# A hybrid decoder step on one core: a unit's output before the next unit's joining, an inversion with fewer DMAs, a projection by halves

## The chip, the core and the metric

One core of a Trainium2 chip runs one launch of the kernel. The metric is device time of that launch in microseconds (us). The engines named below are TensorE (PE, matmul, with its weight loads PEld), VectorE (DVE), ScalarE (ACT), GpSimd (POOL) and SyncE (SP). SyncE and ScalarE issue DMAs, each in the order of its own queue.

## The reference

One layer of a decoder, for a prompt of 1024 tokens and 8 samples of 8 tokens, width 1024. A combined projection `w_in` feeds two mixers: A is RWKV-7 with 8 heads of 64, B a chunked gated delta rule with 4 heads of 128. Their outputs go through `w_o`, a layer norm, a ConvFFN of width 2816, a second layer norm, and a gated embedding of each layer, `p @ w_ple`, with an RMS norm.

```python
proj = x @ w_in
o_a, a_shift_new, a_wkv_new = _rwkv7_mix(proj[..., :A_SHIFT_W], ...)
o_b, b_conv_new, b_ssm_new = _gated_delta_mix(proj[..., A_SHIFT_W:], ...)
mix = jnp.concatenate([o_a, o_b], axis=-1) @ w_o
x = _layer_norm(DN_ALPHA * x + mix, ln1_g, ln1_b)
ffn, f_conv_new = _conv_ffn(x, f_conv, w_up, f_conv_w, f_conv_b, w_down)
x = _layer_norm(DN_ALPHA * x + ffn, ln2_g, ln2_b)
e = _rms_norm(p @ w_ple, ple_g)
x = x + jax.nn.sigmoid(x @ w_ple_gate) * e
```

Both mixers solve, for each chunk of tokens, a lower triangular system with ones on its diagonal: `sol = triangular_solve(eye + Lmat, rhs)`. The kernel inverts these matrices.

## The kernel before

All matrix products are made in three matmuls: each operand is split into a high and a low part (`split`, L257: ScalarE makes the high part at L217, a subtraction at L220 the low one), and high by high, high by low and low by high are accumulated. Weight chunks of 128x512 come from `wchunk` (L385), through the ring `wraw` of 4, on SyncE's queue. The accumulators are four PSUM banks `acc`; mixing uses two banks `aux` and two `scan`. Banks and other rings are given out in the order of the program.

The program is written as one long list, and a scheduler lays it out over the engines' queues ahead of time, by priority and by its own estimate of when each instruction is ready. On the chip each queue then runs strictly in its order. Work written inside `fill()` has a far lower priority: it is taken where nothing else is ready by the estimate.

The mixing is cut into ten units: eight prompt units (tb, half, g), each 256 tokens and one group of heads, numbered 0 to 7 below, and two sample units. A unit passes through these steps:

- `prep` (L1047): loads of the projected rows, convolutions, norms on TensorE (`aux<-tmp,cst`), gram matrices `MG` and `MB`, and at its end `invert`.
- `invert` (L947): 24 matrices of 64x64 per prompt unit. ScalarE's queue (`s.uq`) writes them to DRAM (`inv_t`), then loads the 16x16 diagonal blocks to `iN`, one block per partition, in 4 DMAs (L963). VectorE inverts all 96 blocks at once in 14 steps on `iN`, `iY` and `it`. The result and its transpose go back to DRAM (`inv_x`, `inv_y`), 96 rows of 1 KB each, and from there in 16 DMAs of 16 partitions (L992) to the diagonal blocks of `Dd` and `Dt`, which were cleared once in `setup` (L318).
- `merge` (L996), the joining: four rounds of small matmuls that make the inverse of the 64x64 matrices from the inverted blocks, then three steps that join pairs to 128x128. Each round takes both `aux` banks and begins with `touch` (L204), a matmul of 8 columns that takes the waits of the round (`aux<-zeros`); in rounds 0 and 1 it waits for the loads of `Dt` and `Dd`.
- `scan` (L1069): the chunks one after another, with the state. `scan` gets the joining of the next unit as `ahead` and runs it through `together` in turn with its own steps.
- `mix_out` (L1087): `out` (L899) norms and gates the result, with `aux` banks (`aux<-OA,cst` first), and stores two halves to `od` on SyncE's queue (L928, L934).

The loop in `run` (L1653) goes, for unit i: scan i with the joining of i+1, output i, then `prep` of i+2. Fill: the projections of the second 512 tokens, the embeddings' projection `ple` (L1369), then after unit 3 `dense_first` with `w_o`, which loads `od` of units 0 to 3 and keeps its input order, `norm_first` at normal priority, and the FFN of the first 512 tokens. When the mixing is done, the second 512 tokens and the samples follow, with the FFN in `ffn_second`.

`ple` computes two halves of the columns for each of two blocks of 512 tokens: `dense` runs over 2 weight chunks and 4 token tiles, fills four `acc` banks at once and copies them out at the end. Both `load_x`, `ple`, `ffn_second` and `transposed` put part of the low parts of their splits on GpSimd.

Of the kernel before, what the change touches and what calls it, by code (L numbers as in the profile page):

```python
# [145 lines left out]
class Kern:  # L146
# [109 lines left out]

    def split(s, hi, lo, raw, eng=None):  # L257

        s.act(hi, raw)
        s.tt(lo, raw, hi.bitcast(F32), ALU.subtract, eng or s.nc.gpsimd)  # L260

# [10 lines left out]
    def setup(s):  # L272
# [43 lines left out]
        s.DX = [s.tl([128, 12, LB], "DX%d" % i) for i in range(2)]  # L316
        for t in (s.Dd, s.Dt, *s.DX):
            nc.gpsimd.memset(t, 0.0)  # L318
        for g in range(2):
            for S in (s.SA, s.SB):  # L320
                S.append(s.tl([128, 2, 128], "S%d%d" % (g, S is s.SB)))
                nc.gpsimd.memset(S[g], 0.0)
# [33 lines left out]
    def load_x(s, src, more=None):  # L356

        x = s.xtiles()
        if not more and not s.late:
            for k in range(0, KT, 2):  # L360
                raw = s.tl([128, D], "X", 3, dt=F32R, pool=s.c0).bitcast(F32).rearrange("p (k t) -> p k t", k=2)
                s.nc.sync.dma_start(raw, src[:, k:k + 2, :])
                s.split(x[k // 2][:, 0], x[k // 2][:, 1], raw, s.nc.vector if k < 4 else None)
            return x
        for k in range(KT):
            raw = s.hraw() if s.late else s.st()
            with s.tc.high_priority() if more and k < 1 else ExitStack():
                s.nc.sync.dma_start(raw, src[:, k, :])
                s.split(*s.xk(x, k), raw, s.nc.vector if more else None)
                if more and k % 2 == 0:  # L370
                    more(k)
        return x

    def load_xs(s):
        x = s.tl([128, D], "X", 3, dt=F32R, pool=s.c0).rearrange("p (k i t) -> p k i t", k=KT, i=2)
        raw = s.tmp(128, KT, 64)

        def load(k):
            ks = slice(k, k + 2)
            s.nc.sync.dma_start(raw[:, ks], s.I["xT"][:, ks, T:T + 64])  # L380
            s.split(x[:, ks, 0, :], x[:, ks, 1, :], raw[:, ks], s.nc.vector)

        return x, load

    def wchunk(s, src, to=None):  # L385

        w = src.shape[-1]
        raw = s.wraw()
        hi, lo = to or (s.tl([128, 512], t, 3, dt=F32R, pool=s.mp) for t in ("whi", "wlo"))
        with s.tc.high_priority():  # L390
            s.nc.sync.dma_start(raw[:, :w], src)
            s.split(hi[:, :w], lo[:, :w], raw[:, :w], s.nc.vector)
        return hi, lo
# [545 lines left out]
    def systems(s, sa, sb):  # L939

        for h in range(2):
            r = 64 * h
            yield h, 0, sa["MG"].rearrange("p c a s e t -> p (c a) s e t")[r:r + 64, :, 0, 1 - h, :]
            if r < sb["L"]:
                yield h, 2 * sa["nch"], sb["MB"][r:r + 64, :, :, 0, r:r + 64].rearrange("p q h t -> p (q h) t")

    def invert(s, sa, sb, small):  # L947

        nc = s.nc
        nch = sa["nch"]  # L950
        nb = 2 * sb["nq"]
        nh = 2 * nch + nb
        ns = nh + (2 * nch if small else nh)
        dT = s.tl([64, 24, 64], "inv_t", 2, pool=s.dp)
        d1, d2 = (s.tl([96, 16, 16], t, 2, pool=s.dp) for t in ("inv_x", "inv_y"))
        N, Y, tmp = s.iN, s.iY, s.it
        DX = s.DX[0]
        s.DX = s.DX[::-1]
        for h, y, t in s.systems(sa, sb):
            s.uq.dma_start(dT[:, h * nh + y:h * nh + y + t.shape[1], :], t)  # L960
        n = 4 * ns
        for k in range(4):
            s.uq.dma_start(N[k * ns:(k + 1) * ns], dT[16 * k:16 * k + 16, :ns, 16 * k:16 * k + 16].rearrange("r y t -> y r t"))  # L963
        nc.vector.tensor_copy(Y[:n], N[:n])
        for j in range(1, 15):
            m = 15 - j
            y = Y[:n, 0:j]
            t = tmp[:n, :j * m].rearrange("p (c i) -> p c i", c=j)
            s.mul(t, N[:n, j:j + 1, j + 1:].broadcast_to([n, j, m]), y[:, :, j:j + 1].broadcast_to([n, j, m]))
            s.add(y[:, :, j + 1:], y[:, :, j + 1:], t)  # L970
        nc.vector.memset(Y[:n].rearrange("p a b -> p (a b)")[:, 0::17], 1.0)
        s.uq.dma_start(d1[:n], Y[:n])
        if small:
            nc.gpsimd.memset(DX, 0.0)
            todo = ((DX, d1, 64),)
        else:
            nc.vector.tensor_copy(N[:n], Y[:n].rearrange("p c i -> p i c"))
            s.uq.dma_start(d2[:n], N[:n])
            todo = ((s.Dt, d2, 0), (s.Dd, d1, 0))
        for D, d, w in todo:  # L980
            for h in range(2):
                for k in range(4):
                    rows = slice(64 * h + 16 * k, 64 * h + 16 * k + 16)
                    cols = slice(w * h + 16 * k, w * h + 16 * k + 16)
                    y = k * ns + h * nh
                    if small:
                        s.uq.dma_start(D[rows, :2 * nch, cols], d[y:y + 2 * nch].rearrange("y r t -> r y t"))
                        if h == 0:
                            y += 2 * nch
                            s.uq.dma_start(D[rows, 8:8 + nb, cols], d[y:y + nb].rearrange("y r t -> r y t"))  # L990
                    else:
                        i = s.uq.dma_start(D[rows, :, cols], d[y:y + nh].rearrange("y r t -> r y t"))  # L992
                        sa.setdefault("dma", []).append(i.ins)
        sa["DX"] = sb["DX"] = DX

    def merge(s, sa, sb):  # L996
# [8 lines left out]
        for k in range(4):  # L1005
            bs = [s.bank() for _ in range(2)]
            with s.inrow():
                s.touch(bs[0], s.nc.cur_bb.bb.instructions[-1], *(sa["dma"][8 * k:8 * k + 8] if k < 2 else ()))
                for i in range(12):
# [58 lines left out]

    def scan(s, tb, half, g, st, ahead):  # L1069

# [4 lines left out]
        def a_all():  # L1075
            for c in range(NCH):
                yield from s.a_step(sa, c, OA)
                yield
# [4 lines left out]

        s.together(a_all(), b_all(), *ahead)
        return OA, OB
# [240 lines left out]
    def transposed(s, xs, i, c0, x, tag, dst=None):  # L1326
# [5 lines left out]
        for k in range(0, KT, q):  # L1332
# [18 lines left out]
            s.act(hi, u)  # L1351
            s.tt(lo, u, hi.bitcast(F32), ALU.subtract, s.nc.gpsimd if (k // q) % 2 else None)

# [15 lines left out]
    def ple(s):  # L1369
        nc, I = s.nc, s.I  # L1370
        for tb in range(3):
# [12 lines left out]
            for h in range(2):  # L1384
# [6 lines left out]
                def evac(t, b):  # L1391
# [3 lines left out]

                s.dense(2, (lambda i: x[i]) if x else None, lambda i: I["w_ple"][h][:, i, :], evac,
                        None if x else (lambda i: xs[:, i]), lambda v: out(8, 64, v))

# [210 lines left out]
    def run(s):  # L1609
# [14 lines left out]
        with s.tc.tile_pool(name="c0", bufs=1) as c0:  # L1624
            s.c0 = c0
            with s.tc.tile_pool(name="mix", bufs=1) as p:
# [26 lines left out]
                for i, u in enumerate(units):  # L1653
                    o = s.sample_scan(*u, st[i]) if len(u) == 1 else s.scan(*u, st[i], [s.merge(*st[i + 1][:2])] if len(units[i + 1]) == 3 else [])
                    if len(u) == 1:
                        s.sample_out(*u, st[i], o)
                    else:
                        s.mix_out(*u, st[i], o)
                    if i == 3:
                        with s.fill():  # L1660
# [73 lines left out]
```

## Time and profile before

| | us |
|---|---|
| median of 3 runs (1918.12 to 1926.15) | 1921.58 |
| profiled execution | 1920.4 |
| its span, first to last instruction | 1918.6 |
| TensorE busy in the span | 1831.8 |
| mean granted TensorE clock | 0.989 of full |

The profile is one execution, read by views: the page with busy time of each engine; windows, which give the same for any stretch; waits, which name who waited for whom; and timelines, which give instructions in order of time, with the idle time before each in brackets and what ended it. Times are counted from the span's start. In names, `out<-in` is what an instruction writes and reads; for a matmul the moving operand stands before the stationary one. A `q` behind an engine is its queue, that is a DMA issue there.

### The profile page before, as it was taken

Reading aid. Unit: us, or ns where it says so; the run is one execution under the profiler, and the core shown is the slowest. Engines: PE = TensorE matmul, PEld = TensorE weight load, DVE = VectorE, ACT = ScalarE, POOL = GpSimd, SP = SyncE. Lnnn points to the kernel's source line nnn. Section 1 sums busy time; section 2 is a strip of 40 time slices with the busy share of each in tenths; the row PEclk is TensorE's granted clock in tenths of the full one; section 3 lists DMA queues with packets and bytes.
Section 4 is the critical chain, followed back from the end, with each engine's and each line's share of the span. In section 5 each row is a group of like instructions: output and inputs, shape, how many; then the busy total and the mean of one; then the engine's idle time right before and its main releaser. Section 6 shows DMA issues by size and latency. Waiting matters only on the chain. (4 is left out here: it accounts for less than half of the span.)

```text
span 1918.6 us, 29879 instructions
## 1 busy us (share of the span) xinstructions
PE 1831.8 (95%) x10446; PEld 1463.3 (76%) x10446; DVE 1269.8 (66%) x2748; ACT 918.0 (48%) x1814; POOL 154.7 (8%) x305
## 2 busy tenths in 40 slices
PE   9999999999799798999999999999999999999998
PEld 7878777777567577777887767777787888888877
DVE  4366566758586685877768767666857752455488
ACT  5454447465564744646455435543633332333372
POOL 2000010001000000000000000200212210111000
PEclk9999999999899899999999999999999999999999
DMA  6435342434444365442423446875332222222355
GB/s 216 152 123 153 112 113 89 137 100 133 144 138 145 126 181 163 129 114 82 117 81 112 131 137 194 274 246 200 134 119 92 96 78 83 83 78 79 114 174 165
DMA packets 219126, 255.88 MB, mean 133 GB/s; under 512 B 81848, under 2 KB 117096, under 8 KB 218976
## 3 DMA queue, kind: packets, MB, share of 16 engines
q1 hardware_dynamic: 162040, 246.36, 39.8%
q10 hardware_dynamic: 56936, 7.62, 2.5%
q8 instruction: 82, 1.34, 0.3%
q14 instruction: 68, 0.56, 0.1%
HBM read 200.64 MB, written 53.26 MB: 132 GB/s over the span
## 5 line engine op out<-in xcount | busy, mean ns | idle before, releaser
L190 PE MATMUL acc<-x,whi 128*128 128x512 f32 x2400 | 784.5, 403 | 7.9 <-ACT whi L217 5.1
L220 DVE TENSOR_TENSOR wlo<-wraw,whi 128x512 fp32r<-128x512 f32 (+1 forms) x462 | 323.2, 700 | 343.7 <-ACT whi L217 319.0
L217 ACT ACTIVATE whi<-wraw 128x512 fp32r<-128x512 f32 (+1 forms) x462 | 287.4, 623 | 497.8 <-PE acc L190 169.0
L190 PEld LDWEIGHTS acc<-x,whi 128*128 128x128 f32 x2400 | 429.5, 189 | 89.0 <-issue 7.8
L190 PE MATMUL acc<-x,wlo 128*128 128x512 f32 x1200 | 483.0, 403 | 0.0
L190 PEld LDWEIGHTS acc<-x,wlo 128*128 128x128 f32 x1200 | 226.9, 189 | 54.3 <-issue 6.0
L190 PE MATMUL acc<-whi,X 128*128 128x512 f32 x436 | 145.5, 407 | 9.5 <-ACT st L217 6.2
L217 ACT ACTIVATE st<-acc 128x512 f32<-128x512 f32 (+2 forms) x134 | 77.4, 595 | 62.3 <-PE acc L190 39.2
L190 PEld LDWEIGHTS acc<-whi,X 128*128 128x128 f32 x436 | 81.9, 191 | 29.8 <-ACT st L217 7.2
L190 PE MATMUL acc<-wlo,X 128*128 128x512 f32 x220 | 87.5, 398 | 0.0
L229 DVE SCALAR_TENSOR_TENSOR st<-st,par,st 128x512 f32<-128x512 f32 (+1 forms) x132 | 78.1, 593 | 2.8
L217 ACT ACTIVATE st<-st 128x512 f32<-128x512 f32 x66 | 33.3, 505 | 72.9 <-DVE st L229 68.4
L190 PE MATMUL scan<-whi,X 128*128 128x256 f32 (+2 forms) x208 | 62.4, 335 | 0.0
L217 ACT ACTIVATE tmp<-tmp 128x512 f32<-128x512 f32 (+4 forms) x75 | 40.5, 548 | 30.6 <-DVE tmp L229 22.7
L229 DVE SCALAR_TENSOR_TENSOR st<-st,st 128x512 f32<-128x512 f32 x74 | 40.6, 550 | 19.5 <-ACT st L217 18.6
L190 PE MATMUL scan<-whi,xsm 128*128 128x256 f32 x176 | 49.3, 281 | 2.4 <-ACT st L217 2.4
L190 PE MATMUL scan<-wlo,X 128*128 128x256 f32 (+2 forms) x164 | 51.5, 314 | 0.0
L217 ACT ACTIVATE X<-wraw 128x512 fp32r<-128x512 f32 (+1 forms) x65 | 40.5, 623 | 21.1 <-DMA wraw<-hd 10.7
L506 POOL COPY tail<-st 128x3 f32<-128x3 f32 x52 | 14.6, 283 | 436.6 <-ACT st L217 436.6
L220 DVE TENSOR_TENSOR X<-wraw,X 128x512 fp32r<-128x512 f32 x60 | 43.5, 724 | 9.4 <-ACT X L217 9.3
L217 ACT ACTIVATE tmp<-tmp,par 128x256 f32<-128x256 f32 (+1 forms) x100 | 43.0, 470 | 14.0 <-issue 4.5
L190 PE MATMUL scan<-wlo,xsm 128*128 128x256 f32 x176 | 49.5, 282 | 0.0
(358 smaller groups left out, 3306.9 us busy)
## 6 DMA issues: line engine op xcount, KB each, us to landing
wraw<-w_up SPq DMA_DIRECT2D x176, 256.0 KB
wraw<-w_in SPq DMA_DIRECT2D x112, 256.0 KB
wraw<-w_down SPq DMA_DIRECT2D x98, 256.0 KB
wraw<-hd SPq DMA_DIRECT2D x44, 256.0 KB
wraw<-w_o SPq DMA_DIRECT2D x32, 256.0 KB
wraw<-w_gate SPq DMA_DIRECT2D x32, 256.0 KB
hd<-st SPq DMA_DIRECT2D x22, 256.0 KB
st<-lnv SPq DMA_DIRECT2D x20, 256.0 KB
```

Source lines behind the costliest of these rows:

```text
L190: i = s.nc.tensor.matmul(out, lhsT=lhsT, rhs=rhs, start=start, stop=stop)
L217: s.nc.scalar.activation(out, in_, f, **kw)
L220: (eng or s.nc.vector).tensor_tensor(out, a, b, op)
L229: s.nc.vector.scalar_tensor_tensor(out, a, sc, b, op0, op1)
L506: s.nc.gpsimd.tensor_copy(s.tails[tb][:, f0 + f, :], st[:, TB - 3:TB])
```

## The change

1. The joining of unit i+1 leaves `scan`. It is written behind `mix_out` of unit i, and so behind the output in the program.
2. `invert` uses matrices in DRAM with rows padded to 65 x 64 numbers, so that the four diagonal blocks of all matrices lie at one stride. The blocks are loaded to `iN` in one DMA. For prompt units the result is written in one DMA each for `inv_dd` and `inv_dt`, into diagonal blocks (96 x 16 runs of 64 bytes), and `Dd` and `Dt` are loaded whole, in two DMAs each of 64 partitions and 12 runs of 256 bytes. The parts off the diagonal of `inv_dd` and `inv_dt` are written as zeros in `setup`, by four DMAs on ScalarE's queue from the cleared `DX`; `Dd` and `Dt` are not cleared any more. For sample units only the load to `iN` and the order of blocks change.
3. `ple` takes both weight chunks first, keeps them, and computes token tiles 0 and 1 and then 2 and 3.
4. All splits put their subtraction on VectorE.

```diff
-    def split(s, hi, lo, raw, eng=None):
+    def split(s, hi, lo, raw):
         s.act(hi, raw)
-        s.tt(lo, raw, hi.bitcast(F32), ALU.subtract, eng or s.nc.gpsimd)
+        s.tt(lo, raw, hi.bitcast(F32), ALU.subtract)
...
-        for t in (s.Dd, s.Dt, *s.DX):
+        for t in s.DX:
             nc.gpsimd.memset(t, 0.0)
+        s.dd, s.dt = (s.tl([24, 65 * 64], t, pool=s.dp) for t in ("inv_dd", "inv_dt"))
+        for t in (s.dd, s.dt):
+            for h in range(2):
+                s.uq.dma_start(s.sysrows(t, slice(h, 24, 2)), s.DX[0][64 * h:64 * h + 64, :, 0:64])
...
+    def blocks(s, d, ns):
+        b = d.rearrange("y (k q) -> (y k) q", k=4)[:4 * ns, :16 * 64]
+        return b.rearrange("p (r l) -> p r l", l=64)[:, :, :16]
+
+    def sysrows(s, d, y):
+        return d[y, :64 * 64].rearrange("y (r t) -> r y t", t=64)
...
-        dT = s.tl([64, 24, 64], "inv_t", 2, pool=s.dp)
-        d1, d2 = (s.tl([96, 16, 16], t, 2, pool=s.dp) for t in ("inv_x", "inv_y"))
+        dT = s.tl([24, 65 * 64], "inv_t", 2, pool=s.dp)
...
         n = 4 * ns
-        for k in range(4):
-            s.uq.dma_start(N[k * ns:(k + 1) * ns], dT[16 * k:16 * k + 16, :ns, 16 * k:16 * k + 16].rearrange("r y t -> y r t"))
+        s.uq.dma_start(N[:n], s.blocks(dT, ns))
...
-        s.uq.dma_start(d1[:n], Y[:n])
...
-            nc.vector.tensor_copy(N[:n], Y[:n].rearrange("p c i -> p i c"))
-            s.uq.dma_start(d2[:n], N[:n])
-            todo = ((s.Dt, d2, 0), (s.Dd, d1, 0))
...
-                        i = s.uq.dma_start(D[rows, :, cols], d[y:y + nh].rearrange("y r t -> r y t"))
-                        sa.setdefault("dma", []).append(i.ins)
+        else:
+            nc.vector.tensor_copy(N[:n], Y[:n].rearrange("p c i -> p i c"))
+            for X, d, D in ((N, s.dt, s.Dt), (Y, s.dd, s.Dd)):
+                s.uq.dma_start(s.blocks(d, ns), X[:n])
+                for h in range(2):
+                    i = s.uq.dma_start(D[64 * h:64 * h + 64], s.sysrows(d, slice(h, 24, 2)))
+                    sa.setdefault("dma", []).append(i.ins)
...
-                s.touch(bs[0], s.nc.cur_bb.bb.instructions[-1], *(sa["dma"][8 * k:8 * k + 8] if k < 2 else ()))
+                s.touch(bs[0], s.nc.cur_bb.bb.instructions[-1], *sa["dma"][2 * k:2 * k + 2])
...
-        s.together(a_all(), b_all(), *ahead)
+        s.together(a_all(), b_all())
...
-            s.tt(lo, u, hi.bitcast(F32), ALU.subtract, s.nc.gpsimd if (k // q) % 2 else None)
+            s.tt(lo, u, hi.bitcast(F32), ALU.subtract)
...
-                s.dense(2, (lambda i: x[i]) if x else None, lambda i: I["w_ple"][h][:, i, :], evac,
-                        None if x else (lambda i: xs[:, i]), lambda v: out(8, 64, v))
+                W = [s.wchunk(I["w_ple"][h][:, i, :]) for i in range(2)]
+                s.dense(2, (lambda i: x[i]) if x else None, None, evac, None if x else (lambda i: xs[:, i]),
+                        lambda v: out(8, 64, v), parts=((0, 1), (2, 3)) if x else ((),), kept=W)
...
-                    o = s.sample_scan(*u, st[i]) if len(u) == 1 else s.scan(*u, st[i], [s.merge(*st[i + 1][:2])] if len(units[i + 1]) == 3 else [])
+                    o = s.sample_scan(*u, st[i]) if len(u) == 1 else s.scan(*u, st[i])
                     if len(u) == 1:
                         s.sample_out(*u, st[i], o)
                     else:
                         s.mix_out(*u, st[i], o)
+                    if i + 1 < len(units) and len(units[i + 1]) == 3:
+                        for _ in s.merge(*st[i + 1][:2]):
+                            pass
```

## Rows read from the trace of the kernel before

**Rows 1.** part 1 of the page: busy time, share of the span and instructions per engine

```profile
PE 1831.8 (95%) x10446; PEld 1463.3 (76%) x10446; DVE 1269.8 (66%) x2748; ACT 918.0 (48%) x1814; POOL 154.7 (8%) x305
```

**Rows 2.** windows: stretch, its length, busy time by engine, granted clock, DMA share

```profile
200.00:480.00 280.00, 267.67 (x1784) 213.91 (x1783) 194.48 (x466) 154.19 (x317) 19.61 (x34) 0.99 0.37 114
480.00:760.00 280.00, 240.78 (x1689) 191.45 (x1687) 190.98 (x441) 148.87 (x294) 8.28 (x19) 0.94 0.48 152
760.00:1040.00 280.00, 272.16 (x1758) 214.79 (x1757) 215.84 (x540) 155.81 (x332) 15.92 (x40) 1.00 0.37 104
...
600.00:650.00 50.00, 41.96 (x349) 31.55 (x347) 21.80 (x45) 25.61 (x45) 0.67 (x3) 0.90 0.35 105
```

**Rows 3.** windows, the same view, over the stretches at half clock, with their sum

```profile
520.50:527.40 6.90, 5.82 (x20) 5.13 (x21) 6.38 (x15) 5.18 (x12) 0.00 (x0) 0.51 0.53 194
640.00:650.20 10.20, 7.73 (x25) 5.22 (x26) 5.08 (x10) 9.02 (x17) 0.00 (x0) 0.50 0.55 180
674.10:681.00 6.90, 6.35 (x32) 5.39 (x32) 6.45 (x15) 0.90 (x2) 0.00 (x0) 0.51 0.76 196
sum 34.20, PE 26.94 PEld 22.27 DVE 20.36 ACT 16.54 POOL 0.00; mean PE 5.39 PEld 4.45 DVE 4.07 ACT 3.31 POOL 0.00
```

**Rows 4.** waits of TensorE from 430 to 760: total, times, longest

```profile
PE aux L190 <- DMA Dt<-inv_y: 10.1, 2, 8.4
```

**Rows 5.** timeline of TensorE, 387 to 411: start, busy, instruction, count, idle before

```profile
387.75 0.17 PE L190 MATMUL aux<-zeros 128*128 128x8 f32 x1
...
404.66 1.08 PE L190 MATMUL aux<-OA,cst 128*128 128x512 f32 x2
...
410.67 0.59 PE L190 MATMUL aux<-tmp,cst 128*128 128x512 f32 x1
```

**Rows 6.** timeline of TensorE around unit 3's output

```profile
569.18 0.39 PE L190 MATMUL scan<-AR,S 128*128 128x128 f32 x2
...
628.81 1.08 PE L190 MATMUL aux<-OA,cst 128*128 128x512 f32 x2
...
638.38 1.10 PE L190 MATMUL aux<-tmp,cst 128*128 128x512 f32 x2 [2.54 <-DVE otmp L220]
...
672.74 1.12 PE L190 MATMUL aux<-tmp,cst 128*128 128x512 f32 x2 [3.76 <-DVE tmp L229]
```

**Rows 7.** SyncE's queue, 590 to 712: its longest wait, and its timeline

```profile
SPq L928 <- DVE otmp L220: 20.3, 1, 20.3
...
638.30 0.38 SPq L928 DMA_DIRECT2D od<-otmp  x1
...
640.46 0.33 SPq L1473 DMA_DIRECT2D wraw<-od  x1
```

**Rows 8.** timeline of TensorE, 478 to 525, behind its two longest waits

```profile
489.56 0.34 PE L190 MATMUL aux<-zeros 128*128 128x8 f32 x1 [8.37 <-DMA Dt<-inv_y]
...
521.58 1.22 PE L190 MATMUL acc<-whi,X 128*128 128x512 f32 x2 [5.16 <-ACT st L217]
```

**Rows 9.** timeline of ScalarE and its queue, 454 to 492, unit 3's inversion

```profile
456.49 0.31 ACTq L963 DMA_DIRECT2D iN<-inv_t  x1
...
479.51 0.37 ACTq L972 DMA_DIRECT2D inv_x<-iY  x1
...
483.54 0.32 ACTq L992 DMA_DIRECT2D Dd<-inv_x  x1
484.30 3.77 ACTq L992 DMA_DIRECT2D Dt<-inv_y  x8
...
491.75 1.57 ACT L217 ACTIVATE st<-acc 128x512 f32<-128x512 f32 x3 [9.60 <-DMA Dd<-inv_x]
```

**Rows 10.** timeline of VectorE, the first use of the loaded blocks

```profile
462.92 0.29 DVE L964 COPY iY<-iN 96x256 f32<-96x256 f32 x1 [0.18 <-issue]
```

**Rows 11.** VectorE's costliest group by line; and a wait of TensorE after 1200

```profile
L220 DVE TENSOR_TENSOR wlo<-wraw,whi 128x512 fp32r<-128x512 f32 (+1 forms) x462 | 323.2, 700 | 343.7 <-ACT whi L217 319.0
...
PE acc L214 <- ACT u L217: 2.6, 3, 1.0
```

More of the change, by code (lines that the diff above doesn't have):

```diff
@@ L362, in load_x @@
                 s.nc.sync.dma_start(raw, src[:, k:k + 2, :])
-                s.split(x[k // 2][:, 0], x[k // 2][:, 1], raw, s.nc.vector if k < 4 else None)
+                s.split(x[k // 2][:, 0], x[k // 2][:, 1], raw)
             return x
@@ L368, in load_x @@
                 s.nc.sync.dma_start(raw, src[:, k, :])
-                s.split(*s.xk(x, k), raw, s.nc.vector if more else None)
+                s.split(*s.xk(x, k), raw)
                 if more and k % 2 == 0:
@@ L391, in wchunk @@
             s.nc.sync.dma_start(raw[:, :w], src)
-            s.split(hi[:, :w], lo[:, :w], raw[:, :w], s.nc.vector)
+            s.split(hi[:, :w], lo[:, :w], raw[:, :w])
         return hi, lo
@@ L958, in invert, with of @@
         s.DX = s.DX[::-1]
+        def of(h, y, n):
+            return slice(h * nh + y, h * nh + y + n) if small else slice(2 * y + h, 2 * (y + n) + h - 1, 2)
         for h, y, t in s.systems(sa, sb):
-            s.uq.dma_start(dT[:, h * nh + y:h * nh + y + t.shape[1], :], t)
+            s.uq.dma_start(s.sysrows(dT, of(h, y, t.shape[1])), t)
         n = 4 * ns
-        for k in range(4):
-            s.uq.dma_start(N[k * ns:(k + 1) * ns], dT[16 * k:16 * k + 16, :ns, 16 * k:16 * k + 16].rearrange("r y t -> y r t"))
+        s.uq.dma_start(N[:n], s.blocks(dT, ns))
         nc.vector.tensor_copy(Y[:n], N[:n])
@@ L971, in invert @@
         nc.vector.memset(Y[:n].rearrange("p a b -> p (a b)")[:, 0::17], 1.0)
-        s.uq.dma_start(d1[:n], Y[:n])
         if small:
+            d = s.tl([96, 16, 16], "inv_x", 2, pool=s.dp)
+            s.uq.dma_start(d[:n], Y[:n])
+            d = d.rearrange("(y k) r t -> k r y t", k=4)
             nc.gpsimd.memset(DX, 0.0)
-            todo = ((DX, d1, 64),)
-        else:
-            nc.vector.tensor_copy(N[:n], Y[:n].rearrange("p c i -> p i c"))
-            s.uq.dma_start(d2[:n], N[:n])
-            todo = ((s.Dt, d2, 0), (s.Dd, d1, 0))
-        for D, d, w in todo:
             for h in range(2):
@@ L983, in invert @@
                     rows = slice(64 * h + 16 * k, 64 * h + 16 * k + 16)
[L984 to L991, printed above, removed]
-                        i = s.uq.dma_start(D[rows, :, cols], d[y:y + nh].rearrange("y r t -> r y t"))
-                        sa.setdefault("dma", []).append(i.ins)
+                    y = h * nh
+                    s.uq.dma_start(DX[rows, :2 * nch, rows], d[k, :, y:y + 2 * nch, :])
+                    if h == 0:
+                        s.uq.dma_start(DX[rows, 8:8 + nb, rows], d[k, :, 2 * nch:nh, :])
+        else:
[5 more added lines that the diff above has]
+                    sa.setdefault("dma", []).append(i.ins)
         sa["DX"] = sb["DX"] = DX
@@ L1067, in prep, with scan @@
         return sa, sb, Z
-    def scan(s, tb, half, g, st, ahead):
+    def scan(s, tb, half, g, st):
         sa, sb, Z = st
```

2 lines of the change are left out of this document (1 added, 1 removed).

## Prediction

> **What bounds the kernel now.** I read the engine totals first: TensorE is busy 1831.8 us of 1918.6 [rows 1], so what a change can give back is the 86.8 us in which it has nothing to run, and the time it runs at the lower clock. Next the windows, to see where that lies [rows 2]. Of 280 us each, 200 to 480 leaves TensorE idle for 12.3, 760 to 1040 for 7.8, but 480 to 760 for 39.2, and only there is the mean granted clock 0.94. The clock rows [rows 3] name five stretches at 0.50, the 1.2 GHz level, of 34.2 us together; TensorE is busy for 26.9 us in them, so about 13.5 us go to the clock. All five stand on or just behind a hole. Against its neighbours (about 10 us idle) the stretch loses 29 + 13.5 = 42 us. That is the ground the change can win on. Everywhere else TensorE has fill: projections and FFN matmuls of low priority that run whenever the mixing units leave a gap.
>
> Then the waits of TensorE and its timeline, to see what makes the holes. One is a joining's first touch, 8.37 us for `Dt`, the largest single wait [rows 4, 8]. One is an accumulator of the embeddings' projection that ScalarE had not yet copied out, 5.16 us [rows 8]. The others lie between 603 and 681. Unit 3 ends its scan at 569.6, but its output starts on TensorE only at 628.8 [rows 6]. In between the joining of unit 4 has to be made, which stands ahead in program order and whose inversion is not ready; both take the same two `aux` banks. Unit 1 shows the same order: the joining of unit 2 from 387.8, the output of unit 1 at 404.7, and only then the norms of unit 3, at 410.7 [rows 5]. This late output holds more than itself: SyncE's queue stands 20.3 us at the store of unit 3's output, and the loads of `od` that feed the next fill (`dense_first`, which needs units 0 to 3) come right behind it, from 640.5 on [rows 7]. In that time TensorE waits for norms, 2.54 us the longest [rows 6], that fill would otherwise have covered, and 640 to 650 runs at half clock [rows 3].
>
> **Output ahead of the joining.** The instructions are the same; their order in the program and so on the banks changes. Unit 3's output can start where its scan ends, near 570 to 575, instead of 628.8. Its first store left 638.3 - 628.8 = 9.5 us after that start [rows 6, 7], so it can leave at about 585, and the second behind it. SyncE's queue came to it at 618 (20.3 us before 638.3 [rows 7]), so it need not stand there any more, and `dense_first` finds its input. From 600 to 650 TensorE is idle for 8.0 us [rows 2], and 7.73 busy us at half clock cost 3.9 [rows 3]: 11.9 us at most; I take **10**, since the cause named is removed. Behind it there are 3.76 us before the norms of the next unit [rows 6], and half of 6.35 busy us at the slow clock [rows 3]: 6.9 at most. It is an in-order wait on VectorE with the fill out of accumulators; with the fill shifted it may come or not: **4**, between 0 and 6.9.
>
> The cycle shortens too. Norms of unit u+2 waited for joining, then output; now for the joining alone: 410.7 - 404.7 = 6 us less per unit [rows 5]. That alone gives TensorE nothing, as fill covers it. But over eight units the mixing ends some 50 us earlier, and what fill is left then runs undisturbed. At the idle share around (7.8 of 280 [rows 2]) that is worth 1 us, taken with the small stalls as **2**. For unit 0 the order is worse: its joining partner was made while unit 0 was scanned; now it comes behind the output, by up to 17 us (387.8 to 404.7 is one joining [rows 5]). It delays unit 1 once, in a stretch that has fill (12.3 idle in 280 [rows 2]): **0**; were the cover gone it would cost up to 17.
>
> Queued behind the moved output: on SyncE the two stores and the load of `z` go ahead of the next unit's loads; on ScalarE two table loads and some ten activations now fall into the time in which the inversion of the next unit runs, ahead of its DMA issues. Each can hold an issue by one activation; VectorE's steps of the inversion have the older place in the program and keep priority.
>
> **Fewer DMAs in the inversion.** Per prompt unit, 4 loads of `iN` become 1, the writes stay 2, and 16 loads of `Dd` and `Dt` become 4: 26 issues become 11. The row: ScalarE's queue is taken from 479.51 to 491.65, and the copy of an accumulator behind it had waited 9.60 us [rows 9]. Issues cost 0.47 us each (3.77 for 8). The new path: the write now goes out in 1536 runs of 64 B where it had 96 of 1 KB. Lower bound: as now, 4.0 us from issue to the first dependent issue (479.51 to 483.54 [rows 9]). Upper bound: the four `iN` loads, 1536 runs of 64 B together, 6.4 us from first issue to use (456.49 [rows 9] to 462.92 [rows 10]). Then two issues, 1 us, and a landing: from 1.5 us (the last `Dt` issue ends at 488.07 [rows 9], the touch starts at 489.56 [rows 8]) to 4.0, as the write. `Dt` is there 6.5 to 11.4 us after the write's issue instead of 10.1: 3.6 earlier to 1.3 later; I take 9, since 768 runs are four times what one `Dt` issue moved before. `Dd` follows behind two more issues. ScalarE's burst shrinks from 12.1 us to 6 to 8.4. So the wait for `Dt` at 480.8 is not removed by this, but ScalarE is back 4 to 6 us sooner, and the fill needs it. That hole with its clock is worth 8.4 + 3.5 = 11.9 at most (26.94 busy us at half clock, less the three stretches named in this part, are 7.04 [rows 3]); I take **2**, between -2 and 11.9, by `Dt`, which moves by 1.
>
> First rows, then a rule that speaks against this part: the 1 KB write took 4.0 us [rows 9]. The Trainium skill (DMA: Bandwidth & Descriptors, section Specifications) states that a transfer below 512 B makes the DMA engine read, modify and write. By that the 64 B write lands late, `Dt` with it, and the second rival below becomes likelier; no write of 64 B runs is in this trace, so it is not shown here.
>
> Setup: the zeroed `Dd` and `Dt` are dropped, but four DMAs of 196 KB go out on ScalarE's queue behind the clearing of `DX`. Four issues of 0.47 [rows 9] hold the first splits by 1.9 us at most, and 0.79 MB cross the first loads: 5.2 us at the 152 GB/s of the busiest windows read here [rows 2], if nothing hides them. Between 0 and -7.1: **-2**, since ScalarE has to wait there for its first input anyway.
>
> **Embeddings' projection by halves.** The same matmuls, two accumulators at a time, both weight chunks kept. The hole at 516 to 521.6 [rows 8] comes from four accumulators filled at once and ScalarE late, busy with unit 2's output and the next unit's activations. With halves, two copies can run during the other half's 12 matmuls; and unit 2's output is elsewhere. Hole 5.16 and half of 5.8 busy us at half clock: 8.1 at most; I take **5**.
>
> **Splits on VectorE.** 76 subtractions leave GpSimd. On VectorE one takes 0.70 us at 128x512 [rows 11]: at most 76 x 0.7 = 53 us more over the run, on an engine with 1269.8 of 1918.6 busy [rows 1], mostly in the second half, where TensorE hardly waits. What it can give: transposes that wait for `u`, which waited for GpSimd, 2.6 us [rows 11]. **1**, between 0 and 3; it costs something only if weight splits come late behind them.
>
> **Sum.** 10 + 4 + 2 + 2 + 5 + 1 - 2 = 22, with bounds 44 and -9.1. The profiled execution took 1920.4 (span 1918.6 and 1.8 around it), 1.2 below the median of 1921.6. 1920.4 - 22 = 1898.4, by the median a little more; I write **1898**.
>
> **Rivals.** *The holes move* (0.20). TensorE's order is fixed ahead, and all of it is laid anew. If the fill runs dry elsewhere (the norms after `dense_first` have only two projection groups to cover them), or the output still starts late because its bank is held, some 5 us are left: 1908 to 1925, nearest 1916. For it: two of the five slow stretches aren't tied to the late output. Against: the 20.3 us on SyncE's queue are.
>
> *Each joining waits for `Dt`* (0.11). TensorE's queue is in order; a touch placed by the old estimate holds everything behind it. Before, one of eight waited long (8.37) and one 1.7, 10.1 together [rows 4]. If 64 B writes land late and all eight wait 4 us with 2 more from the clock behind, that is 48 against 22: 1920 + 26 = 1946. It decides from 22/8 = 2.8 us per joining. Against: in six of eight the touch found `Dt` there, so TensorE usually comes later than its plan.
>
> *All of it goes* (0.09). If the whole excess of 42 us and some stalls at other places vanish: 1920 - 55 = 1865.
>
> **Numbers.** The forecast (1872 to 1912) has 0.60. Range 1870 to 1930: it takes in the bounds 44 and -9.1 and leaves out the last two rivals for the most part. Measurement tells 0.5%, 9.6 us, from no change: faster 0.70 (forecast and third rival, with a little of the first), same 0.18, slower 0.12.
>
> **What would show it.** Unit 3's output on TensorE by 580 and the store's wait on SyncE's queue gone: right on the order. Busy share of 480 to 760 above 255 of 280 and clock 0.97 or more: right on the gain. Touches that wait over 3 us for `Dt` in most units: the second rival. TensorE starting after 6 us: the setup is dearer than taken. Wrong if idle time elsewhere grows by what 480 to 760 gives back.

## The result, and the profile after

The changed kernel takes 1904.29 us, median of 4 runs (1897.28 to 1905.65), beside 1919.85 of the kernel before (4 runs, 1916.54 to 1926.15): a ratio of 0.9896 [0.9865, 0.9926], 20 us at the ratio. The forecast was 1898 in a range of 1870 to 1930, faster with a chance of 0.70. The number came out; the way to it did not, as the runs below show. In the tables and sentences below, "idle" is the time in which TensorE runs nothing. The profiled execution took 1903.8, its span is 1901.9 at a mean granted clock of 0.985 (before: 1918.6 at 0.989).

Part 1 of the page after, to be held against [rows 1], and the windows against [rows 2] (stretch, length, busy time of TensorE, weight loads, VectorE, ScalarE, GpSimd, granted clock, DMA share, GB/s):

```profile
PE 1828.2 (96%) x10446; PEld 1468.9 (77%) x10446; DVE 1282.5 (67%) x2824; ACT 921.0 (48%) x1817; POOL 60.5 (3%) x227
...
200.00:480.00 280.00, 273.24 (x1858) 217.68 (x1858) 191.59 (x455) 159.80 (x324) 9.66 (x31) 1.00 0.43 124
480.00:760.00 280.00, 249.79 (x1755) 198.58 (x1753) 206.83 (x491) 166.47 (x327) 5.31 (x16) 0.94 0.52 155
760.00:1040.00 280.00, 269.56 (x1739) 217.17 (x1738) 225.66 (x607) 158.55 (x346) 11.99 (x38) 0.98 0.40 113
...
600.00:650.00 50.00, 43.37 (x374) 36.09 (x373) 27.82 (x56) 28.51 (x59) 1.63 (x6) 0.90 0.44 129
```

TensorE's idle time is 1901.9 - 1828.2 = 73.7 us where it was 86.8, and it is busy for 3.6 us less. From 480 to 760 it is idle for 30.2 us (39.2 before): the hole that the forecast looked at has shrunk, but is not gone, and the clock there is the same 0.94. Busy for 249.8 of 280 at 0.94, it misses the forecast's sign for the gain (above 255, and 0.97 or more). In the window that gave the order's term of 10 us, 600 to 650, it is idle for 6.6 us (8.0 before), again at 0.90. From 760 to 1040 it is idle for 10.4 (7.8), from 200 to 480 for 6.8 (12.3).

TensorE's timeline after, answering to [rows 5, 6, 8] (start, busy, instruction, count, idle before and what ended it):

```profile
12.06 0.55 PE L190 MATMUL acc<-x,whi 128*128 128x512 f32 x1 [2.56 <-ACT x L217]
16.06 0.79 PE L190 MATMUL acc<-x,whi 128*128 128x512 f32 x1 [3.45 <-DVE x L220]
...
499.88 0.38 PE L190 MATMUL aux<-zeros 128*128 128x8 f32 x1 [7.73 <-DMA Dt<-inv_dt]
...
577.62 1.12 PE L190 MATMUL aux<-OA,cst 128*128 128x512 f32 x2 [0.20 <-ACT OA L217]
...
606.88 0.37 PE L190 MATMUL aux<-zeros 128*128 128x8 f32 x1 [4.72 <-DMA Dt<-inv_dt]
```

Unit 3's output starts at 577.6 instead of 628.8, ahead of the joining, whose touch is now at 606.9. SyncE's queue after, to be held against [rows 7]: first its wait at that store, from 540 to 610, then the first store and the first load behind both stores.

```profile
SPq L932 <- DVE otmp L220: 1.1, 1, 1.1
...
588.34 0.38 SPq L932 DMA_DIRECT2D od<-otmp  x1
...
600.61 0.33 SPq L1488 DMA_DIRECT2D wraw<-od  x1
```

The order does what the forecast said: the 20.3 us are 1.1, and the load that stood at 640.5 starts at 600.6. But two things are new. TensorE has two holes between 9.5 and 16.1, right at the start, and its waits for `Dt` have grown (from 200 to 1040, 12.4 of 15.2 us in two touches; [rows 4] had 10.1, 8.4 the longest):

```profile
PE aux L190 <- DMA Dt<-inv_dt: 15.2, 4, 7.7
```

### The profile page after: what moved, and what is told of

Same layout as the page of the kernel before. It is cut to its first block, busy times and chain, and to the rows that moved or that the text cites. A ratio compares the mean times of both kernels' runs of the same rounds, so it can differ in the third digit from the quotient of the medians.

```text
span 1901.9 us, 29626 instructions
## 1 busy us (share of the span) xinstructions
PE 1828.2 (96%) x10446; PEld 1468.9 (77%) x10446; DVE 1282.5 (67%) x2824; ACT 921.0 (48%) x1817; POOL 60.5 (3%) x227
## 4 chain that ended last, share of the span: by engine, by line
PE 78%; DMA 10%; DVE 6%; ACT 3%; issue 2%; ACTq 0%; SPq 0%; DVEq 0%
PE acc L190 48%; PE scan L190 15%; PE aux L190 13%; DMA Dt<-inv_dt 2%; DMA tmp<-gd 1%; PE aux L214 1%; DVE wlo L220 1%; ACT tmp L217 1%; DVE tmp L229 1%; DMA iN<-inv_t 1%; DMA st<-lnv 1%; DMA x2t<-u 1%; ACT whi L217 1%; DVE X L220 1%; DMA wraw<-od 1%
## 5 line engine op out<-in xcount | busy, mean ns | idle before, releaser
L220 DVE TENSOR_TENSOR wlo<-wraw,whi 128x512 fp32r<-128x512 f32 (+1 forms) x462 | 314.1, 681 | 311.1 <-ACT whi L217 280.8
L217 ACT ACTIVATE st<-acc 128x512 f32<-128x512 f32 (+2 forms) x134 | 77.4, 594 | 31.9 <-PE acc L190 27.1
L217 ACT ACTIVATE st<-st 128x512 f32<-128x512 f32 x66 | 33.3, 504 | 67.9 <-DVE st L229 66.3
L220 DVE TENSOR_TENSOR X<-wraw,X 128x512 fp32r<-128x512 f32 (+1 forms) x65 | 44.2, 680 | 9.3 <-ACT X L217 8.9
L190 PEld LDWEIGHTS acc<-wlo,X 128*128 128x128 f32 x220 | 41.9, 191 | 10.8 <-DVE wlo L220 1.6
```

Source lines behind the costliest of these rows:

```text
L190: i = s.nc.tensor.matmul(out, lhsT=lhsT, rhs=rhs, start=start, stop=stop)
L217: s.nc.scalar.activation(out, in_, f, **kw)
L220: (eng or s.nc.vector).tensor_tensor(out, a, b, op)
```

## Experiments

Four parts make the change: the order (O), the splits on VectorE (S), the new inversion with its padded matrices and fewer DMAs (D), the projection by halves (H). Each was put alone into the kernel before and taken alone out of the changed kernel, and the order was paired with each of the others. Each ratio is to the kernel before on the same chip. "us" is the ratio's distance from 1 times 1920.

**Each part alone.** The order:

```
-        s.together(a_all(), b_all(), *ahead)
+        s.together(a_all(), b_all())
...
                         s.mix_out(*u, st[i], o)
+                    if i + 1 < len(units) and len(units[i + 1]) == 3:
+                        for _ in s.merge(*st[i + 1][:2]):
+                            pass
```

> The kernel before with the new order alone: merge runs behind mix_out, everything else as before. Theory (the order carries the gain, by letting the output of a joining fill the next one): 12 to 18 us less than before, about 1905, unit 3's output over by 590 instead of 628.8, and SyncE's wait for the unit's output tile gone. Rival (GpSimd's share of the splits held VectorE up, and its removal carries the gain): within 4 us of before, since the order only moves the same matmuls.

Measured: 1.0018 [1.0001, 1.0035], 3.5 us slower. Here too the output moved forward, to 580.4 from 628.8, and the idle time of 480 to 760 fell from 39.2 to 34.1. But 200 to 480 went from 12.3 to 17.0 and 760 to 1040 from 7.8 to 16.0. The order alone, on which the forecast put 16 of its 22 us, gains nothing: the theory fell in its first run.

The splits:

```
-        s.tt(lo, raw, hi.bitcast(F32), ALU.subtract, eng or s.nc.gpsimd)
+        s.tt(lo, raw, hi.bitcast(F32), ALU.subtract)
...
-            s.tt(lo, u, hi.bitcast(F32), ALU.subtract, s.nc.gpsimd if (k // q) % 2 else None)
+            s.tt(lo, u, hi.bitcast(F32), ALU.subtract)
```

> The kernel before with all splits into two 16-bit halves on VectorE, GpSimd's share gone, nothing else. Theory (the order carries the gain): 0 to 4 us less than before, about 1917. Rival (the splits carry it): 10 to 14 us less, about 1907, nearly all of it in the stretch from 1160 to 1480, where the 512-wide VectorE subtractions that run beside GpSimd's took 1168 ns instead of 688.

Measured: 0.9977 [0.9961, 0.9993], 4.4 us faster. Less than half of what the rival asked, more than the forecast's 1. Nearly all of it lies where the rival looked for it: from 1200 to 1480 TensorE's idle time falls from 11.7 to 7.2 us.

The new inversion:

```
+                s.uq.dma_start(s.sysrows(t, slice(h, 24, 2)), s.DX[0][64 * h:64 * h + 64, :, 0:64])
...
-            s.uq.dma_start(N[k * ns:(k + 1) * ns], dT[16 * k:16 * k + 16, :ns, 16 * k:16 * k + 16].rearrange("r y t -> y r t"))
+        s.uq.dma_start(N[:n], s.blocks(dT, ns))
...
+                    i = s.uq.dma_start(D[64 * h:64 * h + 64], s.sysrows(d, slice(h, 24, 2)))
```

> The kernel before with the new inversion alone: padded matrices, their four zeroing DMAs at the start, the touch of the transposed blocks. Theory (the zeroing DMAs on ScalarE's queue make a hole of some 6 us at the start, and the inversion's fewer DMAs give little back): 2 to 6 us slower than before, about 1924. Rival (fewer DMAs shorten each joining, and the hole at the start comes from elsewhere): 2 to 10 us faster, about 1914, the first 20 us as before.

Measured: 1.0149 [1.0126, 1.0172], 29 us slower, far beyond the theory's 6, with the hole at the start (12.4 us idle before 200, where it was 4.9).

The halves:

```
-                s.dense(2, (lambda i: x[i]) if x else None, lambda i: I["w_ple"][h][:, i, :], evac,
...
+                W = [s.wchunk(I["w_ple"][h][:, i, :]) for i in range(2)]
+                s.dense(2, (lambda i: x[i]) if x else None, None, evac, None if x else (lambda i: xs[:, i]),
+                        lambda v: out(8, 64, v), parts=((0, 1), (2, 3)) if x else ((),), kept=W)
```

> The kernel before with the projection of the embeddings by halves alone. Theory (as forecast, the finer pieces remove waits in the gated MLP's stretch and leave fill for the joinings): 3 to 5 us less than before, about 1916. Rival (the pieces are hidden in either shape): within 2 us of before.

Measured: 0.9995 [0.9977, 1.0012]: nothing, as the rival said. TensorE's waits, by total, show where it went:

```profile
PE aux L190 <- DMA Dt<-inv_y: 11.4, 2, 9.4
PE aux L190 <- DMA Dd<-inv_x: 8.3, 2, 7.6
```

The wait for ScalarE's `st`, 8.4 us in all before and 5.16 the longest [rows 8], is down to 2.1; in its place stand 8.3 us for `Dd`, whose loads ScalarE's queue issues. 480 to 760 is idle for 39.1 us, as before.

The four distances, 3.5 - 4.4 + 28.6 - 1.0, come to 27 us slower. Together the parts are 20 us faster. So nearly all of what happened lies in how the parts act on each other, which a sum of parts cannot hold.

**One part taken out of the changed kernel.** The order put back (`together` with `*ahead`, the three lines behind `mix_out` gone):

```
-        s.together(a_all(), b_all())
+        s.together(a_all(), b_all(), *ahead)
...
-                        for _ in s.merge(*st[i + 1][:2]):
```

> The changed kernel with the order put back: merge runs beside the scans again, as before. Theory (the order carries the gain): 12 us or more of the changed kernel's gain is given back, about 1916 to 1920. Rival (the splits carry it): 1904 to 1908, as the changed kernel.

Measured: 1.0033 [1.0015, 1.0051], 26 us above the changed kernel. In this company the order is worth more than forecast.

The old inversion and set-up back:

```
+        for t in (s.Dd, s.Dt, *s.DX):
...
-        s.dd, s.dt = (s.tl([24, 65 * 64], t, pool=s.dp) for t in ("inv_dd", "inv_dt"))
```

> The changed kernel with the old inversion and no padded matrices. Theory (the zeroing DMAs cost 6 us at the start, the fewer DMAs give back little): 3 to 6 us less than the changed kernel, about 1900, TensorE without its wait at 9.5 to 15.4. Rival (the fewer DMAs shorten each joining by more than the start costs): slower than the changed kernel by 2 to 8 us, about 1909.

Measured: 0.9877 [0.9853, 0.9901], 1898.88 us; 3.6 us below the changed kernel's ratio, though the two intervals overlap, and TensorE's wait between 9.5 and 16.1 is gone (5.0 us idle before 200, 11.4 with it).

GpSimd's share of the splits back:

```
-        s.tt(lo, raw, hi.bitcast(F32), ALU.subtract)
+        s.tt(lo, raw, hi.bitcast(F32), ALU.subtract, eng or s.nc.gpsimd)
```

> The changed kernel with GpSimd's share of the splits put back. Theory (the order carries the gain): 1 to 4 us slower than the changed kernel, about 1907. Rival (the splits carry it): 8 to 12 us slower, about 1914, with the loss in the stretch that answers to 1160 to 1480 of the kernel before.

Measured: 0.9959 [0.9945, 0.9974], 12 us above the changed kernel, as the rival said; but the loss is not where it put it alone: idle from 200 to 480 is 12.8 instead of 6.8, from 760 to 1040 19.5 instead of 10.4, and from 480 to 760 it is 22.3, 7.9 less than with the splits.

**The hole at the start.** The four zeroing DMAs issued by SyncE behind two groups of the projection:

```
-                s.uq.dma_start(s.sysrows(t, slice(h, 24, 2)), s.DX[0][64 * h:64 * h + 64, :, 0:64])
...
+                s.nc.sync.dma_start(s.sysrows(t, slice(h, 24, 2)), s.DX[0][64 * h:64 * h + 64, :, 0:64])
...
-                for _ in range(6):
+                for _ in range(2):
+                    next(pj)
+                s.zero_blocks()
+                for _ in range(4):
                     next(pj)
```

> The changed kernel with the four zeroing DMAs issued by SyncE behind two groups of the projection, instead of by ScalarE at the start. Theory (ScalarE's issues of these DMAs hold up its first evictions, and TensorE with them): TensorE's wait at 9.5 to 15.4 is gone and the time is 4 to 6 us below the changed kernel, about 1899. Rival (the hole is the weights' arrival or VectorE's work at the start): the hole stays, the time stays within 1.5 us of the changed kernel.

Measured: 0.9865 [0.9836, 0.9894], 1898.3 us, 6 us below the changed kernel's ratio; the two intervals overlap, so the profile has to say it. Windows of the changed kernel and of this one:

```profile
0.00:120.00 120.00, 109.44 (x530) 90.87 (x531) 47.67 (x98) 51.95 (x105) 10.14 (x32) 0.97 0.53 173
```

```profile
0.00:120.00 120.00, 115.35 (x563) 94.68 (x563) 50.55 (x104) 59.58 (x116) 9.27 (x32) 1.00 0.56 177
```

33 more matmuls by 120 us, 5.9 us more of TensorE, and no wait but the first in the first 20 us. That the four early DMAs make the hole is shown: in the changed kernel ScalarE issues them at 2.33, 7.50, 8.97 and 10.75, between its first splits. The edit changes two things, though, the queue and the time (SyncE issues them from 21.1 to 38.3), so it does not tell the place on ScalarE's queue from the 0.79 MB beside the first loads.

**Who is the order's partner?** Two parts at a time, each the edits above together. Order and splits:

```
+        s.tt(lo, raw, hi.bitcast(F32), ALU.subtract)
...
+                        for _ in s.merge(*st[i + 1][:2]):
```

> The kernel before with two of the four parts: the new order and all splits on VectorE. The order alone cost 3.5 us, yet taking it out of the changed kernel cost 26, so it needs a partner. Theory (the partner is the split: a GpSimd subtraction stops VectorE for its whole 1.2 to 2.4 us, and with the new order those stops fall into scans): 22 to 28 us less than before, about 1899, the same as without the DMA part, and no VectorE instruction of 1160 to 1480 beside a GpSimd subtraction. Rival (the partner is the projection by halves): 2 to 6 us less than before, about 1920.

Measured: 0.9893 [0.9878, 0.9908], 20.5 us faster: these two parts give as much as all four. The theory's 22 to 28 is missed by a little. Order and halves:

```
+                W = [s.wchunk(I["w_ple"][h][:, i, :]) for i in range(2)]
...
+                        for _ in s.merge(*st[i + 1][:2]):
```

> The kernel before with two parts: the new order and the projection of the embeddings by halves. Theory (the split is the order's partner, the halves do nothing): as the order alone, 2 to 6 us slower than before, about 1928. Rival (the halves are the partner): 15 us or more less than before, about 1908.

Measured: 1.0026 [1.0015, 1.0038], 5 us slower, as the theory said. Order and new inversion:

```
+        s.uq.dma_start(N[:n], s.blocks(dT, ns))
...
+                        for _ in s.merge(*st[i + 1][:2]):
```

> The kernel before with two parts: the new order and the new inversion, GpSimd's share of the splits and the old projection kept. The new inversion alone cost 29 us. Theory (its larger transfers land later, behind the same write, and only where a joining has an output beside it is that covered; of the 29 us the start keeps some 7): 5 to 10 us less than before, about 1916, as the changed kernel with GpSimd's share put back. Rival (the cost of the inversion does not depend on the order): 25 us slower than the order alone, about 1953.

Measured: 0.9967 [0.9952, 0.9982], 6.3 us faster, inside the theory's 5 to 10: the order is worth 35 us with the new inversion beside it. GpSimd's splits are still in this kernel, so the splits are not the order's only partner; added to this pair (the kernel of the next run) they give 2.1 us, inside the two intervals. Last, the changed kernel with the old projection:

```
-                W = [s.wchunk(I["w_ple"][h][:, i, :]) for i in range(2)]
...
+                s.dense(2, (lambda i: x[i]) if x else None, lambda i: I["w_ple"][h][:, i, :], evac,
```

> The changed kernel with the projection of the embeddings as before. Theory (the halves do nothing, as they did nothing alone): within 2 us of the changed kernel's ratio of 0.9896, about 1905. Rival (the halves carry the order): 12 us or more slower than the changed kernel, about 1918.

Measured: 0.9956 [0.9942, 0.9971], 12 us above the changed kernel, the rival's number, though the halves did nothing alone, with the order (5.0 against 3.5) or with order and splits (-23.6 against -20.5).

TensorE's idle time in these runs, us, from the spans, the pages' totals and the windows:

| kernel | us against before | idle in all | 0:200 | 200:480 | 480:760 | 760:1040 | mean clock |
|---|---|---|---|---|---|---|---|
| before | 0 | 86.8 | 4.9 | 12.3 | 39.2 | 7.8 | 0.989 |
| S | -4.4 | 82.1 | 4.8 | 9.2 | 41.3 | 9.2 | 0.990 |
| H | -1.0 | 89.0 | 4.9 | 13.0 | 39.1 | 8.8 | 0.987 |
| O | +3.5 | 91.0 | 4.9 | 17.0 | 34.1 | 16.0 | 0.981 |
| O H | +5.0 | 94.2 | 4.9 | 16.3 | 35.5 | 17.9 | 0.984 |
| O S | -20.5 | 74.3 | 4.9 | 9.4 | 33.3 | 12.2 | 0.986 |
| O S H | -23.6 | 73.1 | 5.0 | 10.3 | 30.8 | 11.6 | 0.986 |
| D | +28.6 | 106.9 | 12.4 | 12.2 | 43.6 | 18.4 | 0.977 |
| D S H | +6.3 | 90.8 | 12.1 | 7.5 | 41.4 | 14.6 | 0.980 |
| O D | -6.3 | 83.3 | 12.2 | 11.7 | 23.8 | 20.2 | 0.984 |
| O D H | -7.9 | 81.6 | 11.0 | 12.8 | 22.3 | 19.5 | 0.987 |
| O D S | -8.4 | 81.9 | 10.4 | 7.1 | 31.9 | 17.7 | 0.982 |
| all four | -20 | 73.7 | 11.4 | 6.8 | 30.2 | 10.4 | 0.985 |
| all, zeroing late | -26 | 68.8 | 6.6 | 7.8 | 31.3 | 7.6 | 0.986 |

Where the order is the only difference (before to O, H to O H, S to O S, D S H to all four, D to O D) the stretch 480 to 760 loses 5, 4, 8, 11 and 20 us of idle time; it is the stretch that the forecast named. Alone the order gives this back, in 760 to 1040 (+8.2) and 200 to 480 (+4.7). The stretches are cut by the clock on the wall, and the kernels do not stand at the same work at the same time, so differences of a few us between neighbours say little; the first column of idle time and the times do.

**What a GpSimd split does.** GpSimd and VectorE in the order alone, around 258 (start, duration, instruction):

```profile
257.83 2.41 POOL L220 TENSOR_TENSOR x<-X,x 128x1024 fp32r<-128x1024 f32 x1 [1.17 <-ACT x L217]
...
257.64 0.17 DVE L220 TENSOR_TENSOR it<-iN,iY 96x26 f32<-96x26 f32 x1
257.85 2.42 DVE L220 TENSOR_TENSOR iY<-iY,it 96x26 f32<-96x26 f32 x1
260.31 0.19 DVE L220 TENSOR_TENSOR it<-iN,iY 96x36 f32<-96x36 f32 x1
...
260.99 1.22 PE L190 MATMUL scan<-S,KN 128*128 128x128 f32 x4 [1.82 <-DVE st L220]
```

A VectorE step of 26 columns, 0.17 us before and 0.19 after it, takes 2.42: as long as the GpSimd subtraction that started 20 ns ahead of it (2.41). `st`, behind it in VectorE's queue, is late by that, TensorE stands 1.82 us in a scan, and from 240 to 280 its granted clock falls to 0.91. With the order and the splits on VectorE, VectorE does the same 128x1024 subtraction itself:

```profile
257.43 0.20 DVE L220 TENSOR_TENSOR iY<-iY,it 96x44 f32<-96x44 f32 x1
257.55 1.22 DVE L220 TENSOR_TENSOR x<-X,x 128x1024 fp32r<-128x1024 f32 x1
258.68 0.20 DVE L220 TENSOR_TENSOR it<-iN,iY 96x50 f32<-96x50 f32 x1
```

It takes 1.22 us instead of 2.41, and TensorE's timeline shows no wait from 250 to 275. In the kernel before the same stop is there (2.45 us at 257.77 for the 44-column step), and TensorE stands behind it too, though its clock from 240 to 280 stays at 1.00:

```profile
261.46 0.66 PE L190 MATMUL scan<-RA,DX 128*128 128x64 f32 x4 [1.99 <-DVE RA L746]
```

So are others: its 17 weight splits `wlo` of 128x512 that ran beside a GpSimd subtraction took 1211 ns in the mean, the 399 with nothing of GpSimd beside them 688. Taken against the same forms alone, VectorE's instructions beside a GpSimd subtraction took 23 us longer in the kernel before, 27 in the order alone.

That these stops are what the splits win beside the order is argued, not shown. Only 11 of the 76 subtractions run before 1100 us, where the mixing is; they cost VectorE 6.5 us there in the kernel before and 11.6 in the order alone, while the splits are worth 24 us beside the order. And the edit does more than remove them: between O and O S the scheduler gives TensorE another order of matmuls from 251 us on, ahead of the first GpSimd subtraction at 254. No run has the new order of the queues with the old engine, or the reverse.

**What fewer DMAs do.** ScalarE's DMA queue (q10: packets, MB, share of the 16 DMA engines) in the second half of unit 3's inversion, before (479 to 492) and after (488 to 501), and then the issues on it after, to be held against [rows 9]:

```profile
q10 hardware_dynamic: 3344, 0.38, 20.2%
```

```profile
q10 hardware_dynamic: 6155, 0.96, 54.7%
```

```profile
488.61 0.31 ACTq L1004 DMA_DIRECT2D inv_dt<-iN  x1
488.96 0.73 ACTq L1004 DMA_DIRECT2D inv_dd<-iY  x1
491.67 1.69 ACTq L1006 DMA_DIRECT2D Dt<-inv_dt  x2
493.40 3.10 ACTq L1006 DMA_DIRECT2D Dd<-inv_dd  x2
```

18 issues became 6, but they carry 2.5 times the bytes, since `Dd` and `Dt` now come with their zeros (192 KB an issue, 4 of them, for 16 of 12 KB), in 1.8 times the packets. After the last `Dt` issue the joining's first matmul came 2.8 us later in the mean of the seven joinings other than unit 1's before, and 5.1 after; from the copy of `iN` it is 11.6 before and 12.6 after. The first half did get shorter: from the last write of `inv_t` to the first use of `iN` it is 9.3 us before and 6.8 after, the 4 loads of `iN` being 1. So of one joining's path 2.5 us are won and 0.9 given back.

## Why the prediction was right, and by which steps it was not

**What bounds the kernel** held: the matmuls are the same 10446 in every run, and what a run won or lost is TensorE's idle time and its clock. For the new inversion alone, the worst run, idle grew by 20.1 us and busy time by 9.6 at the lower clock, 29.7 together, the whole difference of the spans (1948.3 - 1918.6).

**Output ahead of the joining**: the mechanism was right at its place, and the signs named for the order came, the output at 577.6 and SyncE's wait gone; the idle time of 480 to 760 is down by 4 to 20 us in every pair. The sign named for the gain did not come (249.8 busy at 0.94, for 255 and 0.97), and of the 8.0 us idle from 600 to 650, behind the term of 10, the changed kernel keeps 6.6, 4.7 of them now at a touch for `Dt`. The sign of being wrong, idle time that grows elsewhere by what this stretch gives back, came in half: 480 to 760 gives back 9.0 us, the start and 760 to 1040 take 9.1, but 200 to 480 and the time behind 1040 give 13.2 more. The sizes 10 + 4 + 2 were read from the stretch alone. Measured, the same edit is worth +3.5 (slower), +6, -16, -35 and -26 us, alone, beside the halves, beside the splits, beside the inversion, and beside the other three. "TensorE's order is fixed ahead, and all of it is laid anew" stood in the first rival, the holes that move; that rival is what the order alone did, with the gain at its place and the loss at others. It had a chance of 0.20 for the whole change, and the whole change came out 20 us faster all the same.

**Splits on VectorE**: the step that failed worst for its weight. It was costed at 1, between 0 and 3, by one wait of TensorE and by VectorE's busy share. Not seen was that GpSimd's subtraction stops VectorE for its own duration. The row was in reach: [rows 11] has one mean of 700 over 462 `wlo`, two forms and both levels in one number. The part measured 4.4 alone, 24 with the order (1.0018 to 0.9893), 2 with the order and the inversion and 12 in the changed kernel; how much of that is the stops is open. Of the "at most 53 us more on VectorE", 13 appeared (1282.5 after, 1269.8 before), since the 23 us in which it had stood stopped had counted as busy. The Trainium skill (SBUF — State Buffer, section Who interferes with whom) states that a VectorE instruction with two SBUF inputs contends with a GpSimd instruction that reads SBUF, and calls the port pair that the two share an exclusive lock; the 2.42 us at 257.85 agree. Held against the 76 subtractions beforehand, it would have named the term, though not its size.

**Fewer DMAs**: 2 forecast, with -2 as its lower bound. The landing was bounded by 4.0 us after the issue, the write's latency; the touch at 499.88 came 6.5 us after the last `Dt` issue ended, beyond that bound. The prediction counted issues and runs of bytes, not the zeros: it said that 768 runs are four times what an issue moved and took `Dt` as moved by 1 us, and left out that the loads of `Dd` are on the DMA engines at the same time; which of the two makes the touch late was not tried. Alone the part costs 28.6 us, of which the start is 7.5 of idle; with the order it gains 10, with order and splits it costs 12, with halves as well 4. The lower bound of the write, "as now, 4.0 us", was one unit's; over the eight joinings the time from the issue of `iN`'s write to the first load of `Dt` behind it has a median of 2.6 us before (1.85 to 4.84) and 4.0 after (3.06 to 7.23). So the loads behind the write in 64 B runs do start later, by 1.4 us. The packets in the traces give about as much: the two writes are 192 packets of 1 KB at 53 ns before and 3072 of 64 B at 11 ns after, 0.6 and 2.1 us if 16 DMA engines share them evenly (an estimate). The prediction weighed there a sentence of the Trainium skill (DMA: Bandwidth & Descriptors, section Specifications) on transfers below 512 B. The 1.4 us agree with it in sign; whether the lateness is the read-modify-write that it names or the 16 times as many runs is not told apart.

**Setup**: forecast -2 with -7.1 as bound; it is -6 (5.9 us of TensorE by 120). "ScalarE has to wait there for its first input anyway" holds only up to TensorE's first matmul at 4.55 us: the issues at 7.50 to 10.75 stand between splits that TensorE waits for. The sign named for it, TensorE starting after 6 us, missed the hole: it starts at 4.55, as before (4.59), and stops at 9.5.

**Halves**: forecast 5. Alone nothing, with the order 1.5 slower, with order and inversion 1.6 and with order and splits 3 faster, all inside the intervals, and 12 faster only in the full change. The hole at 516 that they were meant to close did close by the halves alone (waits for `st` 8.4 to 2.1), but another opened, for `Dd`.

**The second rival**, each joining waiting for `Dt`, came in part: 15.7 us in five touches of the whole run in place of 10.1 in two, 2.0 per joining over eight, below its deciding 2.8.

**The sum** is what failed as a method. By the runs, the terms would be -3.5, +4.4, -28.6 and +1, 27 us slower; the forecast's were 16, 1, 0 and 5, 22 faster. That the time was met is luck: an order that alone gains nothing and an inversion that alone costs 29 us met in one change, in which the first is worth 26 us and the second costs 4. What stays open is why the order alone gives its gain back, and why either the splits or the inversion stops that: the stops of VectorE at 258 are in the kernel before as well, and which new place each costs was not tried. The rival that fits all the pairs, a queue order that each edit lays anew, was not tested apart from the parts. Nor is it settled why the new inversion loses 21 us beyond its start when the order is missing, and gains 10 when it is there. The idle time says where (760 to 1040, +10.6), and the waits for `Dt` from 200 to 1040 double, from 10.1 to 20.4; the rest of it is spread. The 12 us of the halves in full company stay unexplained too.

The best of the kernels are the changed one with the zeroing late (1898.3 us) and the one without the new inversion (1898.88); they can't be told apart, and both beat the kernel before by 1.2 to 1.35%.

## What to carry to other kernels

Take no part of a re-laid order at its own price: in this kernel, whose TensorE is 95% busy, the same edit was worth anything between +6 and -35 us, by what stood beside it, so measure parts in pairs before keeping or dropping one. An engine that is little busy can still cost another: GpSimd, at 8%, held VectorE for 23 us. Look for instructions of one form whose duration has two levels, and for what ran beside the slow ones. Count a DMA edit in packets and bytes beside its issues; here the joining's first matmul came 2.3 us later behind the last of the fewer issues that carry zeros.

## What the chip showed that was not expected

- A VectorE instruction of two SBUF tensors that starts beside a GpSimd subtraction can wait for its end: 2.42 us instead of 0.19, by what was started 20 ns earlier. `X<-X,st` of 128x512 took 1264 ns beside one (6 times), 680 alone (42). `S<-S,scan`, which reads PSUM, took the same (280 twice beside one, 285 alone).
- It is not `tensor_tensor` alone. In the order alone two `st<-st,par,st` take 2.46 us, 0.75 each alone; the second, of 1.68, starts 0.42 us into GpSimd's subtraction. The 18 in the kernel before that took 755 ns beside a GpSimd subtraction met only the last 0.14 to 0.26 us of one.

```profile
1190.32 2.46 DVE L229 SCALAR_TENSOR_TENSOR st<-st,par,st 128x512 f32<-128x512 f32 x2
...
1190.67 1.55 POOL L220 TENSOR_TENSOR x<-hraw,x 128x512 fp32r<-128x512 f32 x1 [1.29 <-ACT x L217]
```

- A copy of one SBUF tensor was held as well: in the order alone `tmp<-tail`, 128x6, took 1.27 us at 513.81 beside a GpSimd subtraction, 0.17 alone.
- GpSimd can be the one that waits: in the kernel before its `HS<-st,HS` takes 0.33 us with no VectorE instruction beside it (twice), and 0.47 where VectorE's `st<-st,par` had started 0.26 us earlier.
- GpSimd's 128x1024 subtraction takes 2.41 us, VectorE's 1.22; offloading it saves VectorE nothing where VectorE stands for the 2.41.
- From the issue of `iN`'s write to the first load of `Dt` behind it: 1.85 us at the least with 96 runs of 1 KB, 3.06 with 1536 runs of 64 B.
